# Retention's sample queries: weighted states summed by a matrix of ones, in place of a product with the query

## The chip, the cores and the metric

One Trainium2 chip, one of its cores. The time is the device time of one execution of the whole program in microseconds (us); several executions are timed, and their median is given. A core has TensorE (PE; its weight loads are listed as PEld), VectorE (DVE), ScalarE (ACT), GpSimd (POOL) and SyncE (SP), each with an instruction queue of its own that it works through in order. Engines wait for one another by semaphores. SP issues nearly all DMAs here.

## The reference

One step of a decoder layer for a prompt (16 meta tokens and 256 prompt tokens) and for 8 samples that each add one token to a state of their own. The layer is a half feed-forward block, a mixer of two parallel branches (retention with 8 heads, HGRN2 with 16) and a second half feed-forward block. What the change touches is retention of the 8 samples, for which a chunk has one token:

```python
q_dec = q * jnp.exp(lg[:, None] * (idx + 1.0))[:, :, None]
o = jnp.einsum('bhij,bhjv->bhiv', inner, v) + jnp.einsum('bhid,bhdv->bhiv', q_dec, S)
S_new = jnp.exp(lg * C)[:, None, None] * S + jnp.einsum('bhjd,bhjv->bhdv', k_dec, v)
```

With one token both terms of `o` together are the query times the new state: o[v] = sum over d of q[d] * S_new[d, v], with d = 256 features and v = 256 values, for each of 8 heads and 8 samples.

## The kernel before

All matrices are float32. A weight block of 128x128 is split into a high part `whi` (ScalarE's cast, L188) and a low part `wlo` (VectorE's difference, L189), and each product is three matmuls (`xh*whi`, `xl*whi`, `xh*wlo`, L218). Weights come in units of 8 blocks, 512 KB, through three buffers each of `raw`, `whi` and `wlo`: the load of a unit waits for the wlo of the unit three before, and its cast for TensorE's last use of the unit three before.

The mixer's projections run over the heads u = 0 to 7: six groups f, q_h, i_h, q_r, k_r, v_r (names of the parts of `w_in`) of head u, then four gate groups of head u - 1 (`g_r` with `a_r`, `g_h` with `a_h`, for each of two columns of 128). A group is two outputs, 16 k-steps of six matmuls each, four units of weights. When a group's matmuls are issued, `evacuate` takes its result out of PSUM: for a gate group ScalarE makes the sigmoid of `g`, later the sigmoid of `a`, both into tiles named `gs`, and VectorE multiplies them (`gt`, `y`).

Between the k-steps run the two branches as Python generators, `mix_hg(u)` and `mix_ret(u)`. Each `yield n` means: go on n k-steps later (`pump`). TensorE's order is just the order in which the program issues its matmuls; the order of the other engines is set by a scheduler with priorities, in which the weights' casts and differences come first.

`mix_ret(u)` holds the samples' states of a head in four tiles `sms` (tag `smr`), for samples 0 to 3 and 4 to 7 (e) and for both halves of the features (c), each 128 partitions x 4 samples x 256 values. ScalarE scales them by the decay (L1192), VectorE adds key times value (`smr<-vbr,k_r,smr`, L1198), and SP writes them out (`out_srs`). Then, 19 k-steps later for u of 1 and more, TensorE multiplies the states by the queries: `qdr` is a tile of zeros with one query column per sample, 32 columns wide, so that a matmul writes 32 rows of which one is the answer; four samples go side by side into four groups of 32 rows (`tile_position`), into the PSUM tile `pqr`. VectorE's `alone` places the queries in `qdr`. In `mix_hg` the corresponding product `pq` (L1039) is placed by `yield (8, 11, 45)[min(u, 2)]` so that from u = 2 on it comes right before `pqr`. After `pqr` come its centring, and 7 k-steps on the outputs `por` and the normalisation. The first use of the normalised result is in the gate groups of the same head, one round of projections later.

The heads u = 2 to 7 are alike; their `pqr` stands in the third gate group (of head u - 1), after k-step 11. In u = 0 it stands in the group q_r, in u = 1 at the end of the gate groups.

Of the kernel before, what the change touches and what calls it, by code (L numbers as in the profile page):

```python
# [13 lines left out]
AF = mybir.ActivationFunctionType  # L14
ALU = mybir.AluOpType
# [3 lines left out]
P = 128  # L19
# [4 lines left out]
NMETA, SEQ, NS = 16, 256, 8  # L24
# [27 lines left out]
ALONE = 4 * 32 + 1  # L52
# [76 lines left out]
def trunk(ctx: ExitStack, tc: tile.TileContext, A, O):  # L129
    nc = tc.nc  # L130
# [108 lines left out]
    def mul(out, a, b):  # L239
        nc.vector.tensor_tensor(out=out, in0=a, in1=b, op=ALU.mult)  # L240
# [306 lines left out]
    with tc.tile_pool(name="yp", bufs=1) as yp:  # L547
# [7 lines left out]
        with tc.tile_pool(name="mp", bufs=1) as mp:  # L555
# [7 lines left out]
            def tmp(name, shape=(P, T), bufs=1, dt=F32, tag=None):  # L563
                if name in rows:
                    rows[name] = rows[name][1:] + rows[name][:1]
                    return rp.tile(list(shape), dt, tag=rows[name][-1], name=name)
                return mp.tile(list(shape), dt, tag=tag or name, name=name, bufs=bufs)
# [16 lines left out]
            st = {}  # L584
# [5 lines left out]
            qdr = tmp("qdr", (P, 4, ALONE))  # L590
            nc.gpsimd.memset(qdh, 0.0)
            nc.gpsimd.memset(qdr, 0.0)
            qdh_at = [qdh.rearrange("p a c -> p (a c)")[:, 256 * h :] for h in range(2)]
            qdr_at = [qdr.rearrange("p a c -> p (a c)")[:, 2 * ALONE * c :] for c in range(2)]
# [53 lines left out]
            def evacuate(n, c0, c1, o0, o1, b0, b1):  # L648
                if n == "f":
# [6 lines left out]
                    st["f"], st["k"] = f, k  # L656
                elif n == "q_h":
# [4 lines left out]
                    st["q"] = q  # L662
                elif n == "i_h":
# [23 lines left out]
                elif n in ("g_r", "g_h"):  # L687
# [5 lines left out]
                    nc.scalar.activation(sa, o1, AF.Sigmoid)  # L693
                    mul(t, t, sa)
# [38 lines left out]
            def alone(qd, q):  # L733
                nc.vector.tensor_copy(
                    qd[:, :, : 128 : 32].rearrange("p (c e) j -> p c e j", e=2),
                    q[:, :, SEQ:].rearrange("p c (e j) -> p c e j", e=2))
# [9 lines left out]
            def mix_hg(u, f, k, q, v):  # L746

                calm = 2
# [285 lines left out]
                yield (8, 11, 45)[min(u, 2)]  # L1034
# [50 lines left out]
            def mix_ret(u, q, k, v):  # L1085
# [47 lines left out]
                alone(qdr, q)  # L1133
# [70 lines left out]
                yield (11 if u == 0 else 15) + 2 * calm  # L1204
                pq = mx_bank("pqr")
                scores(pq[:, 256:], 2)
                for e in range(2):
                    for c in range(2):
                        for j in range(4):
                            b = 4 * e + j  # L1210
                            nc.tensor.matmul(  # L1211
                                pq[32 * j : 32 * j + 32, :256], qdr_at[c][:, 32 * b : 32 * b + 32],
                                sms[2 * e + c][:, j, :], start=e + c == 0, stop=e + c == 2, tile_position=(0, 32 * j))
# [163 lines left out]
```

## Time and profile before

| | us |
|---|---|
| median of 3 timed runs | 2566.84 (2566.56 to 2567.51) |
| profiled execution, span from first to last instruction | 2563.9 |
| TensorE busy in the span | 2553.4 |
| VectorE busy | 1702.8 |
| ScalarE busy | 1392.2 |
| GpSimd busy | 57.0 |
| mixer, 746 to 1703: VectorE busy of 957 | 776.4 |

The profiled execution has no other time beside its span; the span is 2.9 shorter than the median of the timed runs. In the lines of the profile a row names line, engine, operation, and "written <- read" tiles with shapes (partitions x elements); what stands in brackets at the end of a timeline row is how long the engine had been idle and what released it. TensorE's granted clock is full (1.000) throughout.

### The profile page before, as it was taken

The numbers are of one execution on the slowest core, as the hardware profiler recorded it, in microseconds if no ns is written. First come the engines' busy times: TensorE is split into PE (matmuls) and PEld (weight loads), VectorE is DVE, ScalarE is ACT, GpSimd is POOL, SyncE is SP. The second block draws the span as 40 slices with busy tenths as digits, with TensorE's granted clock in tenths as the row PEclk, the third lists the DMA queues.
The fourth block names the chain that finished last, engine by engine and source line by source line (L and its number), as shares of the span: only waits on it lengthen the run. The fifth ranks groups of instructions, "written<-read, shape, count | busy, mean of one in ns | idle before, by whom it ended". The sixth has DMA issues, their size and how long they took to land.

```text
span 2563.9 us, 56275 instructions
## 1 busy us (share of the span) xinstructions
PE 2553.4 (100%) x23424; PEld 2534.4 (99%) x23424; DVE 1702.8 (66%) x2827; ACT 1392.2 (54%) x2186; POOL 57.0 (2%) x152
## 2 busy tenths in 40 slices
PE   9999999999999999999999999999999999999999
PEld 9999999999999999999999999999999999999998
DVE  6444544475569878777777777777885555556555
ACT  5444444444456767767676666675564444444443
POOL 0000000000000000000000000000000000000000
PEclk9999999999999999999999999999999999999999
DMA  7555555555555876767676767675556565565554
GB/s 244 183 187 183 187 182 184 186 182 186 184 201 180 287 265 232 264 214 260 212 264 215 259 223 255 224 239 188 196 190 197 194 197 195 194 196 195 195 195 149
DMA packets 156897, 536.26 MB, mean 209 GB/s; under 512 B 17952, under 2 KB 25952, under 8 KB 156640
## 3 DMA queue, kind: packets, MB, share of 16 engines
q1 hardware_dynamic: 156352, 532.37, 62.0%
q8 instruction: 183, 3.00, 0.5%
q14 instruction: 74, 0.61, 0.1%
q10 hardware_dynamic: 288, 0.29, 0.0%
HBM read 501.99 MB, written 30.61 MB: 208 GB/s over the span
## 4 chain that ended last, share of the span: by engine, by line
PE 96%; DVE 2%; ACT 0%; issue 0%; DMA 0%; SPq 0%; ACTq 0%; DVEq 0%
PE up L218 36%; PE dn L218 19%; PE pj_i_h L218 3%; PE pj_g_r L218 3%; PE pj_q_h L218 3%; PE pj_g_h L218 3%; PE pj_a_r L218 3%; PE pj_a_h L218 3%; PE pj_f L218 3%; PE pj_q_r L218 3%; PE pj_k_r L218 3%; PE wo L218 3%; PE pj_v_r L218 3%; DVE wlo L189 1%; PE pqr L1211 1%; PE psr L1168 0%
## 5 line engine op out<-in xcount | busy, mean ns | idle before, releaser
L189 DVE TENSOR_TENSOR wlo<-raw,whi 128x1024 fp32r<-128x1024 f32 (+1 forms) x869 | 1062.2, 1223 | 740.7 <-ACT whi L188 737.3
L188 ACT CAST whi<-raw 128x1024 fp32r<-128x1024 f32 (+1 forms) x870 | 905.7, 1042 | 909.2 <-PE up L218 411.0
L218 PE MATMUL up<-xh,whi 128*128 128x280 f32 (+1 forms) x2624 | 725.6, 280 | 0.6 <-ACT whi L188 0.6
L218 PE MATMUL up<-xh,wlo 128*128 128x280 f32 (+1 forms) x2624 | 725.8, 280 | 0.4 <-DVE wlo L189 0.3
L218 PE MATMUL up<-xl,whi 128*128 128x280 f32 (+1 forms) x2624 | 725.4, 279 | 0.0
L218 PEld LDWEIGHTS up<-xh,wlo 128*128 128x128 f32 x2624 | 492.6, 189 | 1.0 <-DVE wlo L189 1.0
L218 PEld LDWEIGHTS up<-xh,whi 128*128 128x128 f32 x2624 | 492.6, 189 | 0.8 <-ACT whi L188 0.8
L218 PEld LDWEIGHTS up<-xl,whi 128*128 128x128 f32 x2624 | 492.6, 189 | 0.0
L218 PE MATMUL dn<-hh,whi 128*128 128x280 f32 (+1 forms) x1376 | 384.7, 280 | 0.0
L218 PE MATMUL dn<-hh,wlo 128*128 128x280 f32 (+1 forms) x1376 | 384.3, 279 | 0.0
L218 PE MATMUL dn<-hl,whi 128*128 128x280 f32 (+1 forms) x1376 | 384.3, 279 | 0.0
L218 PEld LDWEIGHTS dn<-hh,whi 128*128 128x128 f32 x1376 | 260.1, 189 | 0.1
L218 PEld LDWEIGHTS dn<-hl,whi 128*128 128x128 f32 x1376 | 260.1, 189 | 0.1
L218 PEld LDWEIGHTS dn<-hh,wlo 128*128 128x128 f32 x1376 | 260.1, 189 | 0.0
L218 PE MATMUL pj_k_r<-xh,whi 128*128 128x280 f32 x256 | 74.2, 290 | 0.0
L218 PE MATMUL pj_g_r<-xh,whi 128*128 128x264 f32 x256 | 74.0, 289 | 0.0
L218 PE MATMUL pj_v_r<-xh,whi 128*128 128x280 f32 x256 | 73.8, 288 | 0.0
L218 PE MATMUL pj_v_r<-xh,wlo 128*128 128x280 f32 x256 | 72.4, 283 | 0.3 <-DVE wlo L189 0.3
L218 PE MATMUL pj_g_h<-xh,whi 128*128 128x264 f32 x256 | 72.7, 284 | 0.0
L218 PE MATMUL pj_k_r<-xh,wlo 128*128 128x280 f32 x256 | 72.4, 283 | 0.0
L218 PE MATMUL pj_v_r<-xl,whi 128*128 128x280 f32 x256 | 72.3, 283 | 0.0
L218 PE MATMUL pj_k_r<-xl,whi 128*128 128x280 f32 x256 | 72.3, 283 | 0.0
(421 smaller groups left out, 5263.4 us busy)
## 6 DMA issues: line engine op xcount, KB each, us to landing
raw<-in_w_up SPq DMA_DIRECT2D x343, 512.0 KB, 4.1
raw<-in_w_in SPq DMA_DIRECT2D x320, 512.0 KB, 4.3
raw<-in_w_dn SPq DMA_DIRECT2D x172, 512.0 KB, 3.5
smr<-in_sr SPq DMA_DIRECT2D x32, 512.0 KB, 5.0
out_srs<-smr SPq DMA_DIRECT2D x32, 512.0 KB, 6.7
raw<-in_w_out SPq DMA_DIRECT2D x32, 512.0 KB, 3.9
vbr<-vrd SPq DMA_DIRECT2D x32, 256.0 KB, 4.1
smh<-in_sg SPq DMA_DIRECT2D x16, 512.0 KB, 5.2
```

The costliest lines, as they stand in the source:

```text
L188: nc.scalar.copy(hi[:, j:jn, :], raw[:, j:jn, :])
L189: nc.vector.tensor_tensor(out=lo[:, j0:j1, :], in0=raw[:, j0:j1, :], in1=hi[:, j0:j1, :].bitcast(F32), op=ALU.subtract)
L218: nc.tensor.matmul(o, w, t, start=start, stop=stop)
L1211: nc.tensor.matmul(pq[32 * j : 32 * j + 32, :256], qdr_at[c][:, 32 * b : 32 * b + 32], sms[2 * e + c][:, j, :], start=e + c == 0, stop=e + ...
```

## The change

In `mix_ret` the product with the queries is taken apart. The state's rows are weighted by the query before TensorE sees them: for samples 0 to 3 GpSimd multiplies half c = 0 by the query of its feature (a scalar per partition), for samples 4 to 7 ScalarE does; VectorE then multiplies half c = 1 by its query and adds. Both work in place, in the tiles that have been written out. What is left is a sum over 128 partitions, for which TensorE multiplies by a column of ones (`one`, again 32 columns wide): 8 matmuls of the same shape per head in place of 16.

GpSimd first copies one element of the tile `seen` (the output of the evacuation that came last, in the gate groups the sigmoid of `a`) into `lq`, then the queries over it: so the weighting can't begin before that evacuation. The weighting is issued 25 k-steps after the states' writing out, the product 8 k-steps later, 33 in all where there were 19 (15 for u = 0). In `mix_hg`, `pq` moves by the same 14 steps (45 to 59).

```diff
--- before.py
+++ after.py
@@ -587,11 +587,12 @@
 
 
             qdh = tmp("qdh", (P, 4, ALONE))
-            qdr = tmp("qdr", (P, 4, ALONE))
+            one = tmp("one", (P, 2, 32))
             nc.gpsimd.memset(qdh, 0.0)
-            nc.gpsimd.memset(qdr, 0.0)
+            nc.gpsimd.memset(one, 0.0)
+            for e in range(2):
+                nc.gpsimd.memset(one[:, e, e : e + 1], 1.0)
             qdh_at = [qdh.rearrange("p a c -> p (a c)")[:, 256 * h :] for h in range(2)]
-            qdr_at = [qdr.rearrange("p a c -> p (a c)")[:, 2 * ALONE * c :] for c in range(2)]
             vsm = tmp("vsm", (P, P))
             vt2 = tmp("vt2", (P, 2, P))
             scr2 = tmp("scr2", (P, NMETA))
@@ -654,12 +655,14 @@
                         nc.scalar.activation(f[:, j, :], f[:, j, :], AF.Identity, scale=olb[:, c : c + 1], bias=lb[:, c : c + 1])
                     nc.scalar.activation(k, f, AF.Identity, scale=-1.0, bias=1.0)
                     st["f"], st["k"] = f, k
+                    st["seen"] = f[:, 0, :]
                 elif n == "q_h":
                     q = tmp("q", (P, 2, TL))
                     for j, (o, b) in enumerate(((o0, b0), (o1, b1))):
                         nc.scalar.activation(q[:, j, :], o, AF.Sigmoid, **bias(b))
                         mul_biased(q[:, j, :], o, b, q[:, j, :])
                     st["q"] = q
+                    st["seen"] = q[:, 0, :]
                 elif n == "i_h":
                     v = st.pop("i_h", None)
                     if v is None:
@@ -691,6 +694,7 @@
                     mul(t, sg, o0)
                     sa = tmp("gs", (P, TL), bufs=2)
                     nc.scalar.activation(sa, o1, AF.Sigmoid)
+                    st["seen"] = sa
                     mul(t, t, sa)
                     u, e = divmod(c0, 2)
                     while u not in (done_r if n == "g_r" else done_h):
@@ -1031,7 +1035,7 @@
                 if u == 1:
                     yield 2
                     samples(1)
-                yield (8, 11, 45)[min(u, 2)]
+                yield (8, 11, 59)[min(u, 2)]
                 pq = mx_bank("pq")
                 for h in range(2):
                     for b in range(NS):
@@ -1130,7 +1134,6 @@
                         nc.vector.scalar_tensor_tensor(
                             out=lo, in0=x, scalar=g, in1=his[i].bitcast(F32), op0=ALU.mult, op1=ALU.subtract)
                     yield 2
-                alone(qdr, q)
                 vts = [vt[:, 0], vt[:, 1], vs2]
                 vrow = rows_out(vt2.rearrange("p c f -> p (c f)")[16:24, :], 256, "vr")
 
@@ -1201,16 +1204,28 @@
                     for c in range(2):
                         nc.sync.dma_start(O["srs"][u, c, :, 4 * e : 4 * e + 4, :], ss[c])
                     yield 1 if e else 10 if u == 0 else 6
-                yield (11 if u == 0 else 15) + 2 * calm
+                yield 25
+                late_q = tmp("lq", (P, 2, NS))
+                nc.gpsimd.tensor_copy(late_q[:, 0, :1], st["seen"][:, :1])
+                nc.gpsimd.tensor_copy(late_q, q[:, :, SEQ:])
+                for e in range(2):
+                    s0, s1 = sms[2 * e : 2 * e + 2]
+                    for b in range(4):
+                        g = [late_q[:, c, 4 * e + b : 4 * e + b + 1] for c in range(2)]
+                        if e:
+                            nc.scalar.activation(s0[:, b, :], s0[:, b, :], AF.Copy, scale=g[0])
+                        else:
+                            nc.gpsimd.tensor_scalar(out=s0[:, b, :], in0=s0[:, b, :], scalar1=g[0], scalar2=None, op0=ALU.mult)
+                        nc.vector.scalar_tensor_tensor(
+                            out=s0[:, b, :], in0=s1[:, b, :], scalar=g[1], in1=s0[:, b, :], op0=ALU.mult, op1=ALU.add)
+                yield 8
                 pq = mx_bank("pqr")
                 scores(pq[:, 256:], 2)
                 for e in range(2):
-                    for c in range(2):
-                        for j in range(4):
-                            b = 4 * e + j
-                            nc.tensor.matmul(
-                                pq[32 * j : 32 * j + 32, :256], qdr_at[c][:, 32 * b : 32 * b + 32],
-                                sms[2 * e + c][:, j, :], start=e + c == 0, stop=e + c == 2, tile_position=(0, 32 * j))
+                    for j in range(4):
+                        nc.tensor.matmul(
+                            pq[32 * j : 32 * j + 32, :256], one[:, e, :], sms[2 * e][:, j, :],
+                            start=e == 0, stop=e == 1, tile_position=(0, 32 * j))
                 mul(scr2[:NB2], pq[:NB2, 256 : 256 + NMETA], dt[:NB2, c2:])
                 upper_upper_lower(sc2, scr2[:NB2])
                 os = tmp("osr", (P, 256))
```

ScalarE's queue at the end of the third gate group, u = 3 (`whi` with a number is a weight unit's cast, in brackets what the instruction waits for), before:

```order
L1217 COPY osr<-pqr 128x256 [waits PE_49]
L188 CAST whi_15464<-raw_15463 128x8x128 [waits DMAHW7_49,PE_49,Activation_49]
L690 ACTIVATE gs<-pj_g_r_15213 128x264 [waits PE_49]
L188 CAST whi_15494<-raw_15493 128x8x128 [waits DMAHW1_49,PE_49,Activation_49]
L693 ACTIVATE gs<-pj_a_r_15214 128x264 [waits PE_49]
L1055 ACTIVATE sqh<-po 128x256 [waits DVE_49]
```

and with the change:

```order
L188 CAST whi_15427<-raw_15426 128x8x128 [waits DMAHW7_49,DVE_49,PE_49]
L693 ACTIVATE gs<-pj_g_r_15244 128x264 [waits PE_49]
L188 CAST whi_15457<-raw_15456 128x8x128 [waits DMAHW1_49,DVE_49,PE_49]
L696 ACTIVATE gs<-pj_a_r_15245 128x264 [waits PE_49]
L1216 ACTIVATE smr<-smr,lq 128x256 [waits DMAHW0_49,Pool_49]
L1216 ACTIVATE smr<-smr,lq 128x256 x3
L188 CAST whi_15527<-raw_15526 128x8x128 [waits DMAHW3_49,DVE_49,PE_49]
```

The casts around both sigmoids stay where they were; the four products stand behind the second sigmoid and ahead of the next cast, and wait for GpSimd's `lq` and for a DMA that writes states out.

VectorE's queue at the same place, before:

```order
L189 TENSOR_TENSOR wlo_15465<-raw_15463,whi_15464 128x8x128 [waits DMAHW7_49,PE_49,Activation_49]
L240 TENSOR_TENSOR gt<-gs,pj_g_r_15213 128x264 [waits Activation_49]
L189 TENSOR_TENSOR wlo_15495<-raw_15493,whi_15494 128x8x128 [waits DMAHW1_49,PE_49,Activation_49]
L240 TENSOR_TENSOR gt<-gt,gs 128x264 [waits DVE_49,Activation_49]
L742 COPY on_h<-po 128x2x8 [waits PE_49]
L240 TENSOR_TENSOR y<-gt,on_r 128x264 [waits DVE_49]
```

and with the change:

```order
L189 TENSOR_TENSOR wlo_15458<-raw_15456,whi_15457 128x8x128 [waits DMAHW1_49,PE_49,Activation_49]
L240 TENSOR_TENSOR gt<-gt,gs 128x264 [waits DVE_49,Activation_49]
L1219 SCALAR_TENSOR_TENSOR smr<-smr,lq 128x256 [waits DMAHW3_49,Pool_49]
L240 TENSOR_TENSOR y<-gt,on_r 128x264 [waits DVE_49]
L1219 SCALAR_TENSOR_TENSOR smr<-smr,lq 128x256 [waits Pool_49] x3
L189 TENSOR_TENSOR wlo_15528<-raw_15526,whi_15527 128x8x128 [waits DMAHW3_49,PE_49,Activation_49]
L1219 SCALAR_TENSOR_TENSOR smr<-smr,lq 128x256 [waits DMAHW0_49]
L1219 SCALAR_TENSOR_TENSOR smr<-smr,lq 128x256 x3
L189 TENSOR_TENSOR wlo_15593<-raw_15591,whi_15592 128x8x128 [waits DMAHW4_49,PE_49,Activation_49]
```

The eight sums come behind gt, four ahead of a unit's wlo and four behind it; a sum of the first four waits for GpSimd's product.

TensorE's queue around the sample products of u = 3, before (third gate group, after k-step 11, `xh_10` being the eleventh chunk of x):

```order
L218 MATMUL pj_a_r_15214<-xh_10_9275,wlo_15277 128x264
L1039 MATMUL pq<-smh,qdh 32x128 [waits DMAHW5_49]
L1039 MATMUL pq<-smh,qdh 32x128 x7
L1039 MATMUL pq<-smh,qdh 32x128 [waits DMAHW1_49]
L1039 MATMUL pq<-smh,qdh 32x128 x7
L1141 MATMUL pqr<-q_r,k_r 16x16 x2
L1211 MATMUL pqr<-smr,qdr 32x256 x16
L218 MATMUL pj_g_r_15213<-xh_11_9279,whi_15276 128x264
```

and with the change (fourth gate group, after k-step 9, one k-step into the unit whose cast stood between the two sigmoids):

```order
L218 MATMUL pj_a_h_15376<-xh_8_9269,wlo_15458 128x264
L1043 MATMUL pq<-smh,qdh 32x128 [waits DMAHW5_49]
L1043 MATMUL pq<-smh,qdh 32x128 x7
L1043 MATMUL pq<-smh,qdh 32x128 [waits DMAHW1_49]
L1043 MATMUL pq<-smh,qdh 32x128 x7
L1144 MATMUL pqr<-q_r,k_r 16x16 x2
L1226 MATMUL pqr<-smr,one 32x256 [waits DVE_49] x8
L218 MATMUL pj_g_h_15375<-xh_9_9273,whi_15457 128x264
```

Both products moved together by 14 k-steps, half of the retention matmuls are gone, and the others wait for VectorE.

## The prediction

> **What bounds the kernel now.** I read the page first: span, busy shares, chain.
>
> ```profile
> span 2563.9 us, 56275 instructions
> PE 2553.4 (100%) x23424; PEld 2534.4 (99%) x23424; DVE 1702.8 (66%) x2827; ACT 1392.2 (54%) x2186; POOL 57.0 (2%) x152
> PE 96%; DVE 2%; ACT 0%; issue 0%; DMA 0%; SPq 0%; ACTq 0%; DVEq 0%
> ```
>
> TensorE is the bound for nearly the whole span. The list of TensorE's own waits (total, times, longest) says how little the others have held it up so far: nine rows, 4.4 us together, of which these are the first two and the last.
>
> ```profile
> PE pw L515 <- DVE eps_h L163: 1.0, 1, 1.0
> PE pt L1116 <- POOL tails L1103: 0.9, 1, 0.9
> ...
> PE wo L218 <- DVE yl L226: 0.2, 1, 0.2
> ```
>
> So a microsecond of TensorE's work taken away is won, and a microsecond for which TensorE is made to wait is lost. The change does both, once a head. The profiled span of 2563.9 us is 2.9 (0.1%) below the median of 2566.84, and I add my sum to the median. Less than 0.2%, 5.1 us, can't be told from no change here.
>
> Next I took one head apart, the fourth (u = 3), in the timelines (start, duration, what). TensorE:
>
> ```profile
> 1190.44 0.28 PE L218 MATMUL pj_a_r<-xh,wlo 128*128 128x264 f32 x1
> 1190.65 1.08 PE L1039 MATMUL pq<-smh,qdh 128*32 128x128 f32 x32
> ...
> 1191.60 0.42 PE L1211 MATMUL pqr<-smr,qdr 128*32 128x256 f32 x3
> ...
> 1193.47 0.38 PE L218 MATMUL pj_g_r<-xh,whi 128*128 128x264 f32 x1
> ...
> 1196.28 0.28 PE L218 MATMUL pj_g_r<-xh,whi 128*128 128x264 f32 x1
> ...
> 1196.95 0.28 PE L218 MATMUL pj_g_h<-xh,whi 128*128 128x264 f32 x1
> ```
>
> The HGRN2 sample product (`pq`) and the retention one (`pqr`) stand side by side in the third of the four gate groups; one k-step of six matmuls lasts 0.67 (1196.28 to 1196.95); the fourth gate group begins at 1196.95. ScalarE and VectorE at the same place:
>
> ```profile
> 1191.48 1.05 ACT L188 CAST whi<-raw 128x1024 fp32r<-128x1024 f32 x1 [1.41 <-DMA raw<-in_w_in]
> ...
> 1194.94 1.05 ACT L188 CAST whi<-raw 128x1024 fp32r<-128x1024 f32 x1 [0.23 <-DMA raw<-in_w_in]
> 1196.81 0.39 ACT L690 ACTIVATE gs<-pj_g_r 128x264 f32<-128x264 f32 x1 [0.83 <-PE pj_g_r L218]
> 1197.39 1.04 ACT L188 CAST whi<-raw 128x1024 fp32r<-128x1024 f32 x1 [0.19 <-DMA raw<-in_w_in]
> 1198.35 0.38 ACT L693 ACTIVATE gs<-pj_a_r 128x264 f32<-128x264 f32 x1
> ```
>
> ```profile
> 1198.47 1.23 DVE L189 TENSOR_TENSOR wlo<-raw,whi 128x1024 fp32r<-128x1024 f32 x1 [0.81 <-ACT whi L188]
> 1199.61 0.43 DVE L240 TENSOR_TENSOR gt<-gt,gs 128x264 f32<-128x264 f32 x1
> ...
> 1200.08 0.43 DVE L240 TENSOR_TENSOR y<-gt,on_r 128x264 f32<-128x264 f32 x1
> 1200.43 0.16 DVE L240 TENSOR_TENSOR sqh<-on_h 128x8 f32<-128x8 f32 x1
> ```
>
> Three weight casts in a row were released by a DMA's landing and not by TensorE: the weight stream is late here. The table by stretch says why (its last cells are clock, share of the DMA engines' time, GB/s), and so do the issues with their median time to landing, first of 1178 to 1202 us, then of the whole run: the sample states come in and go out at this place, and a weight load takes 5.8 us against 4.3.
>
> ```profile
> 1190.00:1202.00 12.00, 12.00 (x147) 10.85 (x146) 8.23 (x18) 6.50 (x15) 0.00 (x0) 1.00 0.95 335
> ```
>
> ```profile
> raw<-in_w_in SPq DMA_DIRECT2D x8, 512.0 KB, 5.8
> ...
> raw<-in_w_in SPq DMA_DIRECT2D x320, 512.0 KB, 4.3
> ```
>
> **The matmuls removed.** Sixteen per head become eight of the same shape. Sixteen last from 1191.60 to 1193.47, 1.87 us; half is 0.93, and all of it is TensorE's path. Eight heads: **-7.4 us**.
>
> **When TensorE asks for the sums.** With `pq` and `pqr` gone from the third gate group (1190.55, where the step ended, to 1193.47: 2.92 us), TensorE begins the fourth group at 1196.95 - 2.92 = 1194.03. Nine steps follow (9 x 0.67 = 6.03), then `pq` and the scores as before (1190.55 to 1191.60: 1.05). It asks for the first four sums at 1201.1, and half of 0.93 later, at **1201.6**, for the last four.
>
> **When they are ready.** GpSimd's first new copy waits for the sigmoid of `pj_a_r` (the tile `seen`). In ScalarE's new order that sigmoid still stands behind the weight cast which the DMA released at 1197.39, and the DMA doesn't land sooner because TensorE is early: its issue hangs on earlier wlos, which hang on earlier landings. So the sigmoid ends at 1198.73 as now. That is 4.7 after the new start of the fourth group, when TensorE has done seven of the nine steps; 2.9 us are left to 1201.6. What must still pass, in VectorE's new order, is the rest of this wlo and gt (to 1200.04), one sum, y, three sums, the next unit's wlo, four sums. Sums of this shape exist, back to back:
>
> ```profile
> 1298.91 2.07 DVE L1198 SCALAR_TENSOR_TENSOR smr<-vbr,k_r,smr 128x256 f32<-128x256 f32 x5 [1.27 <-ACT smr L1192]
> ```
>
> Five in 2.07 is 0.40 from start to start. A wlo takes 1.14 to the next start (1198.47 to 1199.61), y 0.35 (1200.08 to 1200.43). Eight sums, y and wlo are 8 x 0.40 + 0.35 + 1.14 + 0.1 at the end = 4.8 us of VectorE alone, more than the 2.9 that are left. ScalarE's four products (as long as a sigmoid of 264 columns, 0.38) run beside the first sums, with the cast for that wlo behind them in its queue, and are no later than the wlo's turn.
>
> GpSimd's product of 128x256 is not in the trace. Its nearest rows, and one that tells more, with VectorE's row of the same moment:
>
> ```profile
> 745.21 0.53 POOL L591 MEMSET qdh<- 128x516 f32 x1 [743.95 <-PE dn L218]
> ...
> 832.22 0.28 POOL L1174 TENSOR_SCALAR gam<-sro 128x1 f32<-128x1 f32 x1
> ...
> 1296.51 1.18 POOL L1174 TENSOR_SCALAR gam<-sro 128x1 f32<-128x1 f32 x1 [9.91 <-ACT sro L1170]
> ```
>
> ```profile
> 1296.43 1.21 DVE L189 TENSOR_TENSOR wlo<-raw,whi 128x1024 fp32r<-128x1024 f32 x1
> ```
>
> A memset of twice the columns takes 0.53, so 256 columns are worth some 0.2, and with 0.28 for one column I take 0.45. But that same one-column instruction takes 1.18 when a wlo runs, and ends at 1297.69, just behind the wlo's 1297.64: GpSimd is held while VectorE reads.
>
> Three prices for this head follow.
> - Free: first product done at 1199.7, VectorE starts its sums right after gt, at 1200.04, and ends at 1204.9; TensorE waits 1204.9 + 0.1 - 1201.6 = 3.4.
> - Copies held: the copy that falls into wlo and gt ends with them, at 1200.1, the second at 1200.4, the first product at 1200.85; plus 4.8 is 1205.7: a wait of 4.2.
> - All held: products and sums also exclude each other, so 4 x 0.45 stands in one line with VectorE's first five: 1200.4 + 1.8 + 1.95, wlo 1.14, four sums 1.7: 1207.0, a wait of 5.5.
>
> I take the middle one: the row at 1296.51 shows a small instruction held, and no row shows a 128x256 one that holds or is held. For the other five late heads (u = 2 and 4 to 7), whose order is the same, this is how far the cast may come sooner; ScalarE's row and the issue of its load in u = 2:
>
> ```profile
> 1070.76 1.04 ACT L188 CAST whi<-raw 128x1024 fp32r<-128x1024 f32 x1
> ```
>
> ```profile
> 1064.37 0.33 SPq L185 DMA_DIRECT2D raw<-in_w_in  x1
> ```
>
> 1064.37 + 5.8 = 1070.2, so TensorE's lead would bring the cast forward by 0.6 at most. With half of that, six heads wait 3.9 each: **+23.4 us** (ends, from free less 0.7 to all held: +16 and +33).
>
> The Trainium skill goes further than the row at 1296.51. The page "SBUF — State Buffer", section "Who interferes with whom", says that a VectorE instruction with two SBUF inputs and a GpSimd instruction that reads SBUF contend for one port, and the later one is blocked in full. The trace agrees as far as it goes (1.18 against 0.28). By that rule every new product stands against every new sum: "all held", below.
>
> **The first two heads.** In the first (u = 0) `seen` is long done, but ScalarE's products wait until the states of samples 4 to 7 are written out, and a weight cast waits behind them:
>
> ```profile
> 854.47 0.80 SPq L1202 DMA_DIRECT2D out_srs<-smr  x1
> ...
> out_srs<-smr SPq DMA_DIRECT2D x32, 512.0 KB, 6.7
> ```
>
> ```profile
> 859.89 1.05 ACT L188 CAST whi<-raw 128x1024 fp32r<-128x1024 f32 x1 [0.83 <-DMA raw<-in_w_in]
> ```
>
> 854.47 + 6.7 = 861.2; four products, two copies, cast from some 863.3 instead of 859.89. TensorE has about two units of weights (2.7 us each) ahead of it there, which covers part: +1.5 (ends 0 and 2.5). In the second head (u = 1) fourteen steps lie between the last gate group and the sums instead of nine, 3.4 us more: 0.
>
> **Smaller edits.** VectorE loses eight small copies (`alone`) and gains 64 x 0.40 = 26 us; outside these places its 66% leave gaps. GpSimd's memsets come before the projections. `pq` and both normalisations move by 14 steps; the gates that use them come 80 steps or more after the sums, in the last head 4 to 12 after the norms. On SP's queue the next head's two state loads now wait for the last sums; behind them are weight loads that are needed three units later, which covers 1.6 us.
>
> **The sum.** 2566.84 - 7.4 + 23.4 + 1.5 = 2584.3.
>
> **Rivals.** Hidden (the other side): the sums are done when TensorE comes, 2566.84 - 7.4 = 2559.4. It needs the sigmoid about 4 us sooner, so weights that land as if no states moved beside them; it decides at a wait of 0.93 a head. For it: eight sums are only 3.2 us, and 2 or 3 units are buffered. Against: three casts in a row released by DMAs that were issued long before. Even: weights land up to 2 us sooner and no copy is held, waits of 0.5 to 2 in six heads and none in the first: 2562 to 2572. All held: 2566.84 - 7.4 + 33 + 2.5 = 2595; for it speaks 1.18 against 0.28. Each product behind a whole wlo, as at 1296.51: beyond 2600; against it, only one wlo stands among them. That the eight matmuls save nothing is not likely: nothing else fills TensorE between 1191.60 and 1193.47.
>
> **How the numbers follow.** Forecast (2572 to 2590) 0.56; all held 0.17; beyond 2600 0.04; even 0.12; hidden 0.11. Slower by over 0.2% is the first three, 0.77; within 0.2% is even, 0.12; faster is hidden, 0.11. The range 2567 to 2600 leaves out hidden, the lower part of even and the last: under 0.2.
>
> **What would show it.** A new row among TensorE's waits, `pqr` L1226 on VectorE `smr`, six times or more at about 4 us; `pqr` itself 0.9 a head; GpSimd's copy of `seen` drawn out over the wlo; the cast ahead of the sigmoid still released by a DMA. If these casts follow TensorE at once, "when they are ready" is wrong and 2560 to 2572 comes out; if GpSimd's products take 1 us and more, "all held" or worse.

## The result, and the profile after

The changed kernel takes 2610.07 us (median of 4, 2609.76 to 2613.35), the kernel before 2566.70 beside it: a ratio of 1.0172, 95% interval 1.0157 to 1.0186. It is slower, as forecast, but by 43 us and not by 17.5. The profiled execution's span is 2608.5, 44.6 more than before. The page of the changed kernel: span, busy shares, chain.

```profile
span 2608.5 us, 56165 instructions
PE 2574.9 (99%) x23296; PEld 2539.2 (97%) x23296; DVE 1733.4 (66%) x2883; ACT 1402.3 (54%) x2216; POOL 100.3 (4%) x202
PE 85%; DVE 6%; DMA 4%; ACT 2%; POOL 1%; issue 1%; SPq 0%; ACTq 0%; DVEq 0%; POOLq 0%
```

VectorE, DMA, ScalarE and GpSimd now hold 13% of the chain, where they had 2%. TensorE is listed as busier although it has less to do; that is told below (the clock). Its own waits and, in the second fence, those of its weight loads (total, times, longest):

```profile
PE pqr L1226 <- DVE smr L1219: 9.1, 18, 0.9
PE pj_q_r L218 <- ACT whi L188: 4.8, 1, 4.8
PE pst L1026 <- DVE km L255: 2.3, 1, 2.3
PE pj_f L218 <- DVE wlo L189: 2.0, 2, 1.4
```

```profile
PEld pqr L1226 <- DVE smr L1219: 26.0, 44, 1.4
```

The forecast row is there, and most of it stands with the weight loads: the `one` columns for each matmul are loaded only when the sum is ready. (The two rows overlap in time and must not be added.) The next rows were not forecast; they are single waits in the first two heads, of which only 0.7 of the last row was there before.

Some names in these and later rows: `osr` is the copy of the result `pqr` that VectorE centres, and `por` turns it; `pst` is a product of the HGRN2 branch that reads `km`, which VectorE makes; `pt` turns small tiles, among them `ends`, which GpSimd copies.

To divide the 44.6 us I take the start of the same matmul in both traces, the first of the third gate group ahead of the sums, or of the very last group. Before:

```profile
924.63 0.28 PE L218 MATMUL pj_g_r<-xh,whi 128*128 128x264 f32 x1
...
1056.79 0.28 PE L218 MATMUL pj_g_r<-xh,whi 128*128 128x264 f32 x1
...
1749.85 0.28 PE L218 MATMUL pj_g_h<-xh,whi 128*128 128x264 f32 x1
```

and with the change:

```profile
933.80 0.28 PE L218 MATMUL pj_g_r<-xh,whi 128*128 128x264 f32 x1
...
1072.18 0.28 PE L218 MATMUL pj_g_r<-xh,whi 128*128 128x264 f32 x1
...
1794.42 0.28 PE L218 MATMUL pj_g_h<-xh,whi 128*128 128x264 f32 x1
```

The lag is 9.2 us after head 0, 15.4 after head 1 and 44.6 at the end: **15.4 us in the first two heads, 29.2 in the six late ones.** The same two lags of every experiment stand in the table of the next section.

**A late head** (u = 3), in the timelines of GpSimd, ScalarE, VectorE and TensorE:

```profile
1218.24 0.95 POOL L1209 COPY lq<-gs 128x1 f32<-128x1 f32 x1 [25.50 <-ACT gs L696]
...
1219.64 3.69 POOL L1218 TENSOR_SCALAR smr<-smr,lq 128x256 f32<-128x256 f32 x4
...
1216.84 1.05 ACT L188 CAST whi<-raw 128x1024 fp32r<-128x1024 f32 x1 [1.17 <-DMA raw<-in_w_in]
1217.79 0.38 ACT L696 ACTIVATE gs<-pj_a_r 128x264 f32<-128x264 f32 x1
...
1217.92 1.23 DVE L189 TENSOR_TENSOR wlo<-raw,whi 128x1024 fp32r<-128x1024 f32 x1 [0.94 <-ACT whi L188]
...
1220.60 0.69 DVE L1219 SCALAR_TENSOR_TENSOR smr<-smr,lq 128x256 f32<-128x256 f32 x1 [1.11 <-POOL smr L1218]
...
1223.36 0.48 DVE L1219 SCALAR_TENSOR_TENSOR smr<-smr,lq 128x256 f32<-128x256 f32 x1 [0.21 <-POOL smr L1218]
1223.77 1.22 DVE L189 TENSOR_TENSOR wlo<-raw,whi 128x1024 fp32r<-128x1024 f32 x1
1224.90 1.67 DVE L1219 SCALAR_TENSOR_TENSOR smr<-smr,lq 128x256 f32<-128x256 f32 x4
...
1221.39 0.60 PE L1226 MATMUL pqr<-smr,one 128*32 128x256 f32 x2
...
1225.43 1.81 PE L1226 MATMUL pqr<-smr,one 128*32 128x256 f32 x8 [0.91 <-DVE smr L1219]
1227.17 0.38 PE L218 MATMUL pj_g_h<-xh,whi 128*128 128x264 f32 x1
```

The sigmoid (`gs`) ends at 1218.17; only then can GpSimd's copy of it begin, and behind it the products. The four products take 0.92 from start to start (3.69 for four), each of the first four sums waits for its product, the wlo follows, then the last four sums, which end at 1226.57. TensorE is ready at 1221.39. Without a wait the projection would have gone on 0.93 later, at 1222.3; it went on at 1227.17: 4.9 us lost.

**Head 0**, GpSimd, SP, ScalarE and TensorE:

```profile
851.74 5.32 POOL L1218 TENSOR_SCALAR smr<-smr,lq 128x256 f32<-128x256 f32 x4 [1.22 <-DMA out_srs<-smr]
857.01 1.11 POOL L773 COPY smh<-acch 128x1 f32<-128x1 f32 x1
...
858.15 0.33 SPq L774 DMA_DIRECT2D smh<-in_sg  x1
858.59 0.37 SPq L185 DMA_DIRECT2D raw<-in_w_in  x1
859.00 0.43 SPq L1205 DMA_DIRECT2D out_srs<-smr  x1
...
865.36 1.71 ACT L1216 ACTIVATE smr<-smr,lq 128x256 f32<-128x256 f32 x4 [5.49 <-DMA out_srs<-smr]
...
867.77 1.05 ACT L188 CAST whi<-raw 128x1024 fp32r<-128x1024 f32 x1
...
868.88 0.59 PE L218 MATMUL pj_q_r<-xh,whi 128*128 128x264 f32 x1 [4.83 <-ACT whi L188]
```

and the same copy of one column before, then SP's wait for it in the changed kernel:

```profile
851.89 0.30 POOL L769 COPY smh<-acch 128x1 f32<-128x1 f32 x1 [18.11 <-DVE acch L836]
```

```profile
SPq L774 <- POOL smh L773: 7.1, 1, 7.1
```

Five links: GpSimd's products hold back a one-column copy; SP's load of an HGRN2 state waits for that copy; behind it on SP stand a weight load and the writing out of the states; ScalarE's products wait for the writing out; the weight cast stands behind them.

**The clock.** The table by stretch, 1 us each (TensorE busy first; after the engines the granted clock):

```profile
867.00:868.00 1.00, 0.00 (x0) 0.00 (x0) 0.68 (x3) 1.00 (x4) 0.25 (x1) 0.75 1.00 360
868.00:869.00 1.00, 0.12 (x1) 0.13 (x1) 0.94 (x3) 1.00 (x2) 0.00 (x0) 0.50 1.05 430
...
873.00:874.00 1.00, 1.00 (x6) 1.00 (x6) 0.97 (x4) 0.95 (x5) 0.00 (x0) 0.50 0.86 119
874.00:875.00 1.00, 1.00 (x10) 1.00 (x9) 0.94 (x4) 0.39 (x2) 0.00 (x0) 0.84 0.76 287
...
974.00:975.00 1.00, 1.00 (x6) 0.85 (x5) 0.80 (x3) 0.98 (x2) 0.00 (x0) 0.50 0.46 123
```

The granted clock falls to 0.50 at 867.5, still in the stall, and stays there until 874.3: 6 matmuls start in a us instead of 10 to 12. That is why TensorE "gains" busy time. Some 5 us of these were work at half clock, so 2.5 us are lost. In head 1 the idle time is 1.4 (wlo) and 2.3 (`pst`, whose km stands on VectorE behind five sums, 970.10 to 972.16, and a wlo); the clock is at half from 973.3 to 980.1, about 3.2 lost.

### The profile page after: what moved, and what is told of

The parts are those of the page before. It is cut to its first block, busy times and chain, and to the rows that moved or that the text cites. A ratio compares the mean times of both kernels' runs of the same rounds, so it can differ in the third digit from the quotient of the medians.

```text
span 2608.5 us, 56165 instructions
## 1 busy us (share of the span) xinstructions
PE 2574.9 (99%) x23296; PEld 2539.2 (97%) x23296; DVE 1733.4 (66%) x2883; ACT 1402.3 (54%) x2216; POOL 100.3 (4%) x202
## 4 chain that ended last, share of the span: by engine, by line
PE 85%; DVE 6%; DMA 4%; ACT 2%; POOL 1%; issue 1%; SPq 0%; ACTq 0%; DVEq 0%; POOLq 0%
PE up L218 36%; PE dn L218 18%; PE pj_v_r L218 3%; PE wo L218 3%; PE pj_q_h L218 3%; PE pj_f L218 3%; PE pj_q_r L218 3%; PE pj_i_h L218 3%; PE pj_k_r L218 3%; DMA raw<-in_w_in 3%; DVE wlo L189 3%; PE pj_g_r L218 2%; PE pj_a_r L218 2%; PE pj_g_h L218 1%; PE pj_a_h L218 1%
## 5 line engine op out<-in xcount | busy, mean ns | idle before, releaser
L218 PE MATMUL pj_g_h<-xh,wlo 128*128 128x264 f32 x256 | 71.2, 278 | 1.9 <-DVE wlo L189 1.9
```

The source lines that it names most:

```text
L218: nc.tensor.matmul(o, w, t, start=start, stop=stop)
```

## The experiments

Lags as above, from the profiled executions; medians and ratios from the timed runs. A profiled execution of a kernel with long waits can lie some us from its median (f4: span 2599.9, runs 2601.68 to 2608.21), and a lag of one profile is no better than some 3 us: f1, f4, h3 and h5 leave the late heads as in the changed kernel and show 25.9 to 27.0 where that shows 29.2. In f1, h2 and h5 1.3 to 1.6 us of the lag given for heads 0 and 1 are there at 745 us already, ahead of the mixer's first matmul.

| kernel | median us | ratio, 95% interval | heads 0, 1 | heads 2 to 7 |
|---|---|---|---|---|
| changed | 2610.1 | 1.0157 to 1.0186 | 15.4 | 29.2 |
| e1 ones alone | 2562.3 | 0.9972 to 0.9991 | -0.4 | -2.6 |
| e2 move alone | 2573.7 | 1.0016 to 1.0035 | 4.8 | 2.9 |
| h4 ones, moved | 2572.1 | 1.0009 to 1.0028 | 5.4 | -1.5 |
| f1 late heads only | 2594.3 | 1.0089 to 1.0119 | 1.9 | 27.0 |
| f2 first heads only | 2581.4 | 1.0037 to 1.0071 | 16.6 | 0.2 |
| e3 products on VectorE | 2618.2 | 1.0186 to 1.0217 | 13.6 | 39.7 |
| e4 no copy of seen | 2589.2 | 1.0074 to 1.0104 | 11.9 | 10.3 |
| g1 short products | 2596.7 | 1.0098 to 1.0128 | 11.4 | 19.6 |
| h2 no copy, short | 2584.4 | 1.0048 to 1.0082 | 11.3 | 8.4 |
| h1 no sums | 2597.3 | 1.0105 to 1.0135 | 10.3 | 19.8 |
| f3 late ask | 2602.1 | 1.0125 to 1.0155 | 13.6 | 21.8 |
| g5 late ask, short | 2592.8 | 1.0084 to 1.0115 | 9.9 | 13.4 |
| g4 three together | 2595.2 | 1.0092 to 1.0125 | 8.6 | 21.9 |
| g3 next gate, heads 2 to 6 | 2574.9 | 1.0021 to 1.0043 | 0.7 | 7.0 |
| f4 first heads later | 2607.5 | 1.0137 to 1.0168 | 9.2 | 26.8 |
| h3 head 0 without ScalarE | 2607.8 | 1.0144 to 1.0174 | 15.3 | 25.9 |
| h5 head 0, copies moved | 2605.5 | 1.0133 to 1.0167 | 14.1 | 26.5 |

**What the parts make without the weighting.** e1: no weighting, old places.

```diff
-                yield (8, 11, 59)[min(u, 2)]
+                yield (8, 11, 45)[min(u, 2)]
...
-                yield 25
-                late_q = tmp("lq", (P, 2, NS))
...
-                yield 8
+                yield (11 if u == 0 else 15) + 2 * calm
```

> The weighting is left out: the 8 matmuls by ones sum the states as they are, at the place of before (so the sample outputs lack the query). Only the matmuls removed and the eight small copies of alone are left of the change. Late sums (my theory: the loss is all waiting for the weighting, the matmuls themselves save 0.93 a head): 2566.8 - 7.4 = 2559.4, 2557.5 to 2561. Rival, the saved matmuls are worth nothing because the weight stream limits TensorE at that place: 2566 to 2568.

It is faster by 4.8 us (0.9981): each head gains 0.87, and some is given back, since TensorE then meets weights that are late (two waits of the gate groups for wlo, 1.2 us in all). e2: only the places, in the kernel before.

```diff
-                yield (8, 11, 45)[min(u, 2)]
+                yield (8, 11, 59)[min(u, 2)]
...
-                yield (11 if u == 0 else 15) + 2 * calm
+                yield 33
```

> The kernel before with nothing but the two places moved: pqr 33 steps after the states' writing out, pq by yield 59; 16 matmuls with the queries as before. Late sums: the move alone costs nothing, 2566.8, 2565 to 2570. Rival, the place: pq and pqr no longer give the weight loads 2.9 us in the third gate group, TensorE runs into the weights there, and most of the 43 us would be there without the weighting: 2585 or more. Between: 1.7 and 1.2 us that the third group of two heads lost in the changed kernel, 2570 to 2573.

It is 6.6 us slower: neither nothing nor most of the 43, and just above the case between. The first two heads carry 4.8 of 7.7. (The 1.7 and 1.2 us of the changed kernel that are named above stand in the second gate group of two heads, not in the third.) h4 has both parts.

```diff
-                yield 25
-                late_q = tmp("lq", (P, 2, NS))
...
-                yield 8
+                yield 33
```

> Eight matmuls by ones and both places moved as in the changed kernel, no weighting (the query is left out). Both parts add up: 2567.1 - 4.9 (matmuls alone) + 6.6 (move alone) = 2568.8, 2566 to 2572. Rival (the move's cost came from 16 matmuls at the new place, and eight fit): 2562 to 2565.

The result is 2572.1, 4.7 above before and at the upper end of the range: the parts add up within 3 us, and the eight matmuls don't pay for the move. In head 0 `por` waits 3.1 us for `osr`, and the clock is at half for 3.4 us from the end of that wait. The weighting itself thus costs 2610.1 - 2572.1 = 38 us.

**Which heads.** Weighting for some heads, the others with queries and old places (f1 as shown, f2 with `u < 2`).

```diff
+                weigh = u >= 2
...
-                yield 25
+                yield 25 if weigh else (11 if u == 0 else 15) + 2 * calm
```

> The change for the heads 2 to 7 only; heads 0 and 1 keep the 16 matmuls with the queries at their old places. By the starts of the groups in the changed kernel's trace the heads 2 to 7 make 29.2 of its 44.6 us: 2566.8 + 29.2 = 2596, 2590 to 2600. Rival (my prediction's share: the first two heads cost 1.5 less 1.9, everything lies in the late heads): 2608 or more.

> The change for the heads 0 and 1 only; heads 2 to 7 as before. By the changed kernel's trace these two make 15.4 us, of which some 9.3 are TensorE idle (weights behind ScalarE's products in head 0, km behind VectorE's sums in head 1) and some 6.7 half clock after it, less 1.9 for the matmuls: 2566.8 + 15.4 = 2582, 2577 to 2586. Rival (my prediction's share): 2566 to 2569.

They lose 27.2 and 14.3 us: 41.5 of 43.4, so the two shares add up within 2 us, and the first two heads are a third of the loss. The rival, my prediction's share, falls.

**Who paces a late head.** e3: GpSimd's products to VectorE.

```diff
-                            nc.gpsimd.tensor_scalar(out=s0[:, b, :], in0=s0[:, b, :], scalar1=g[0], scalar2=None, op0=ALU.mult)
+                            nc.vector.tensor_scalar(out=s0[:, b, :], in0=s0[:, b, :], scalar1=g[0], scalar2=None, op0=ALU.mult)
```

> GpSimd's four products a head go to VectorE, all else as in the changed kernel. Late sums: a product of 128x256 with one input takes VectorE 0.3 to 0.4 (between its copy of 16 columns, 0.17, and its two-input 0.40 to 0.48) in place of 0.92 on GpSimd, the four products no longer set the pace of the first four sums, and in a late head the last sum ends about 1 us sooner: -6; in the second head GpSimd's copy for km is no longer behind the products: -2 to -6 with the half clock behind it. 2596 to 2603. Rival (the pace is not GpSimd's, only the place or the late sigmoid counts): 2608 to 2613, slower if anything since VectorE does more.

The expectation was wrong: it is 8 us slower than the changed kernel, though a product takes 0.35. The group of the products, and VectorE's timeline of u = 3:

```profile
L1218 DVE TENSOR_SCALAR smr<-smr,lq x32: 344/349/356, 853.4 to 1756.2; 128x256 f32<-128x256 f32 x32
```

```profile
1221.38 1.22 DVE L189 TENSOR_TENSOR wlo<-raw,whi 128x1024 fp32r<-128x1024 f32 x1 [0.66 <-ACT whi L188]
1222.53 0.48 DVE L1219 SCALAR_TENSOR_TENSOR smr<-smr,lq 128x256 f32<-128x256 f32 x1
...
1223.98 1.22 DVE L189 TENSOR_TENSOR wlo<-raw,whi 128x1024 fp32r<-128x1024 f32 x1
1225.11 1.27 DVE L1219 SCALAR_TENSOR_TENSOR smr<-smr,lq 128x256 f32<-128x256 f32 x3
```

Two sums stand ahead of this; the scheduler put one wlo ahead of the third sum and a second among the others; with a wait of 0.66 for a cast the last sum ends at 1226.38, hardly sooner. In u = 2 and from u = 4 on the waits are longer (up to 1.7 in one piece, against 0.9), and the clock falls there: five stretches at 0.50, 23.9 us in all (from 1356.6 to 1363.4, for instance), in which TensorE worked for some 22 us and so lost 11. That is as much as the 10.5 by which the late heads are slower than in the changed kernel. So e3 doesn't tell what GpSimd's pace costs: its products add to VectorE's work, and the clock covers the rest. e4: without the copy of `seen`, the gate that holds the weighting until the sigmoid.

```diff
-                nc.gpsimd.tensor_copy(late_q[:, 0, :1], st["seen"][:, :1])
```

> GpSimd's copy of the tile seen is left out, so the weighting of samples 0 to 3 may begin when their states are written out (landed at 1210.2 in the fourth head, where the sigmoid ended at 1218.2), the other four when theirs are (1218.0). Late sums: the first four are done before TensorE comes, the last four end near 1221 instead of 1226.6; five of the late heads' 5 us go, the first two heads stay: 2610 - 24 to 30, 2580 to 2586. Rival, a new block: ScalarE's products wait for the DMA of the written states with a weight cast behind them, as in the first head, and TensorE waits for weights instead: 2600 or more.

The time falls by 20.8 us, that of the late heads from 29.2 to 10.3: the result lies between the two ranges, nearer the first, and of all single edits this one brings most. In head 1, too, `pst` now waits 0.5 at most instead of 2.3, and the half clock there is gone. What is left is a new wait, as the rival had it but in size far smaller:

```profile
PE pj_g_r L218 <- DVE wlo L189: 7.7, 6, 2.7
```

g1: the products shortened, nothing else.

```diff
-                            nc.gpsimd.tensor_scalar(out=s0[:, b, :], in0=s0[:, b, :], scalar1=g[0], scalar2=None, op0=ALU.mult)
+                            nc.gpsimd.tensor_scalar(out=s0[:, b, :32], in0=s0[:, b, :32], scalar1=g[0], scalar2=None, op0=ALU.mult)
```

> The changed kernel with GpSimd's products on 32 of the 256 columns (the weighting of the other 224 is left out for samples 0 to 3, half c = 0); every other instruction stays. GpSimd's pace: the products take about 0.3 in place of 0.92, the first four sums follow at 0.40 instead of 0.92, the wlo behind them and the last four sums come 1.5 to 2 us sooner in each of six late heads: 2610 - 9 to 12, 2598 to 2601. Rival (VectorE's own queue and the casts are the limit, as the products on VectorE at 0.35 brought nothing): 2607 to 2611.

The time falls by 13.4 us, 9.6 of it in the late heads: GpSimd's pace costs 1.6 a head (1.0 if the changed kernel's late heads are put at 25.9, as in h3). This is the first theory, with a result a little below its range. h2 has both edits.

> The copy of seen left out and GpSimd's products on 32 of 256 columns. Without the copy TensorE waited 7.7 us for wlo in the third group of the six late heads. GpSimd's pace (that wlo stands behind sums that wait for products of 0.92): most of that goes, 2589 - 5 to 8, 2581 to 2584. Rival (that wlo waits for a cast behind ScalarE's products, which wait for the written states' DMA): 2587 to 2590.

The result is 2584.4, 4.8 below e4 and just above the first theory's range. The wait for wlo in the third group falls from 7.7 to 3.3, but that in the fourth group rises from 1.3 to 3.8; the late heads gain only 1.9, which is within the scatter of one profile. So what the pace costs with the gate gone is not settled. h1: no sums on VectorE.

```diff
-                        nc.vector.scalar_tensor_tensor(
-                            out=s0[:, b, :], in0=s1[:, b, :], scalar=g[1], in1=s0[:, b, :], op0=ALU.mult, op1=ALU.add)
```

> The changed kernel without VectorE's 64 sums (half c = 1 is left out of the sample outputs); TensorE waits for the products alone. Sums on VectorE: in a late head the last product ends at 1223.3 where the last sum ended at 1226.6, 3.1 less for six heads, and no wlo stands behind sums; in head 1 km no longer stands behind five sums, another 4 to 7: 2610 - 19 - 4 to 7 = 2584 to 2588. Rival (GpSimd and its gate alone): 2600 or more.

The result is 2597.3, between the theories and nearer the rival. Even with no sum to make, gate and GpSimd alone keep 19.8 of the 29.2.

**A later place.** f3: the matmuls 12 steps later.

```diff
-                yield 8
+                yield 20 if 2 <= u < HR - 1 else 8
```

> The changed kernel with the eight matmuls 12 k-steps (8 us) later in the heads 2 to 6; the weighting itself stays where it is. Late sums (TensorE waits only because it asks 5 us before VectorE has the last sum): five heads lose their wait, 2610 - 25 = 2585, 2582 to 2592. Rival (the engines' queues are what is short, so that TensorE waits for wlo or the casts instead, wherever pqr stands): 2600 or more.

It gains only 8.0, and the rival is right in kind. TensorE's wait for the sums is left in head 7 alone (1.5), but two other rows have come; the timelines of u = 3 show the first (ScalarE's casts, then VectorE):

```profile
PE pj_g_h L218 <- DVE wlo L189: 8.0, 7, 1.7
PE pt L882 <- POOL ends L755: 4.7, 5, 0.9
```

```profile
1218.40 1.98 ACT L188 CAST whi<-raw 128x1024 fp32r<-128x1024 f32 x2
...
1220.57 0.48 DVE L1219 SCALAR_TENSOR_TENSOR smr<-smr,lq 128x256 f32<-128x256 f32 x1 [0.21 <-POOL smr L1218]
1220.97 1.22 DVE L189 TENSOR_TENSOR wlo<-raw,whi 128x1024 fp32r<-128x1024 f32 x1
```

The first cast was done at 1219.43; its wlo starts at 1220.97, since it stands behind four sums that GpSimd paces. Most of the loss only changed its place. g5 is f3 with short products:

> GpSimd's products on 32 of 256 columns and the matmuls 12 k-steps later in the heads 2 to 6. GpSimd's pace: in the late-ask kernel TensorE waited for a wlo that stood behind the four paced sums (cast done 1219.43, wlo 1220.97 in the fourth head); with short products that wlo comes at once, and five heads lose most of what they still wait: 2602 - 8 to 15, 2587 to 2594. Rival (the late ask left what VectorE's and the DMA's load cost there): 2600 to 2603.

It is 9.3 below f3, the late heads fall from 21.8 to 13.4, and the wait of `pj_g_h` for wlo from 8.0 to 1.3: that reading holds. g4 is e4, f4 (below) and f3 together:

> Three of the edits together: no copy of seen, the first two heads later (10 and 6 steps), the matmuls 12 steps later in heads 2 to 6. If each works on its own wait: 2610 - 21 (seen) - 3 to 9 (first heads) = 2580 to 2586, the late ask adding 0 to 5 more, since without the copy TensorE waits for wlo in the third group and not for the sums: 2576 to 2586. Rival (the gains add up, 21 + 3 + 8): 2573 to 2578, still slower than before.

The expectation was wrong: it is 6 us slower than e4 alone. The edits don't add; with the matmuls later, the late heads lose 21.9 instead of 10.3. Its rows for wlo in the third group (8.1 us), for `pt` (4.7) and for head 0's cast (5.0) stand side by side; why head 0's stall and a half clock in head 2 came with them stays open. g3: heads 2 to 6 only, weighted behind the last sigmoid of the round, summed in the next (the edit is shown against the changed kernel).

```diff
+                weigh = 2 <= u < HR - 1
...
-                yield 25
+                yield 41 if weigh else (11 if u == 0 else 15) + 2 * calm
...
-                yield 8
+                if weigh:
+                    yield 20
```

> The change for the heads 2 to 6 only, weighted one evacuation later (behind the last sigmoid of the round, where the states have long landed) and summed by TensorE in the next round; heads 0, 1 and 7 as before, pq as before. If all is a matter of the place, where states and weights share the DMA and VectorE's wlo is what TensorE waits for: 2567 - 5 x 0.87 = 2562.7, 2560 to 2566. Rival (GpSimd's pace ahead of wlo costs wherever it stands, 1.5 a head): 2568 to 2574.

```profile
PE pj_q_h L218 <- DVE wlo L189: 4.3, 5, 0.9
```

It is 7.8 us slower than before: the rival, a little beyond its range. The written states have long landed here, though SP issues the next head's two state loads in the midst of it (1220.5 in u = 3), and TensorE still waits for a wlo in each of the five heads. At none of the three places (third group, fourth, next round) does the weighting pass unseen, and no version that computes all of it beats the kernel before.

**Head 0's chain.** f4: weighting and matmuls later in heads 0 and 1.

```diff
-                yield 25
+                yield 35 if u == 0 else 31 if u == 1 else 25
```

> The changed kernel with weighting and matmuls 10 k-steps later in head 0 and 6 later in head 1. Blocked queue (in head 0 ScalarE's products wait for the DMA of the written states and the weight cast waits behind them; in head 1 the sums stand ahead of km on VectorE): by then the states are out and km is done, the idle 9.3 and the half clock behind it go, what the move itself costs stays: 2596 to 2601. Rival (the first two heads are short of engines, not badly ordered; the block comes at another cast): 2605 to 2612.

In the profiled execution the first two heads lose 9.2 instead of 15.4, with head 0's stall down from 4.8 to 1.8 and no half clock behind it; the median of the runs fell by 2.6 only. So the first theory holds in kind for head 0, and its size is not decided. For head 1 it fails: the products still follow the sigmoid, `pst` waits 2.3 as before, and the half clock stays (966.8 to 973.6). h3: head 0 without ScalarE's products.

```diff
-                        if e:
+                        if e and u:
                             nc.scalar.activation(s0[:, b, :], s0[:, b, :], AF.Copy, scale=g[0])
```

> In head 0 alone GpSimd does all eight products and ScalarE none; the rest as changed. Blocked queue (ScalarE's first product waits for the DMA of the written states, 865.3, with a weight cast behind it): TensorE's 4.8 us and the 3.3 of half clock go, 2610 - 8 = 2602, 2598 to 2606. Rival (the wait passes on: GpSimd's copies for the states of HGRN2 now stand behind its products): 2607 to 2612.

The result is 2607.8, the rival in kind: the wait passed on to VectorE's wlo, behind sums that now wait for GpSimd:

```profile
PE pj_q_r L218 <- DVE wlo L189: 5.8, 1, 5.8
```

So ScalarE's place is a link and not the first. h5: in head 0 the one-column copies leave GpSimd's queue.

```diff
-                    nc.gpsimd.tensor_copy(sms[h][:, 0, :1], kts[0][:, 0, :1] if h else acc[:, 15:16])
+                    (nc.gpsimd if u else nc.vector).tensor_copy(sms[h][:, 0, :1], kts[0][:, 0, :1] if h else acc[:, 15:16])
...
-                    nc.gpsimd.tensor_copy(vbs[h][:, 0, :1], kts[1][:, 0, :1] if h else acc[:, 2 * P + 15 : 2 * P + 16])
+                    (nc.gpsimd if u else nc.vector).tensor_copy(vbs[h][:, 0, :1], kts[1][:, 0, :1] if h else acc[:, 2 * P + 15 : 2 * P + 16])
```

> In head 0 alone the four one-column copies (L773, L777) for which SP's loads of the HGRN2 states wait go from GpSimd to VectorE; the rest as changed. GpSimd's queue as the head of the chain (products 851.74 to 857.06, the copy behind them, SP's load waiting for it 7.1 us, behind that on SP a weight load and the writing out, for which ScalarE's products wait, with a weight cast behind them): SP is 4 to 5 us sooner, TensorE's 4.8 and the 3.3 of half clock behind it go, 2610 - 8 = 2602, 2599 to 2605. Rival (SP's queue is not the head; the states' writing out is late for VectorE's sake): 2608 to 2612.

SP's wait and TensorE's, in the first heads:

```profile
SPq L774 <- DVE smh L773: 2.1, 1, 2.1
```

```profile
PE pj_q_r L218 <- ACT whi L188: 2.0, 1, 2.0
```

7.1 became 2.1 and 4.8 became 2.0: the copy behind GpSimd's products is the first link. The median fell by 4.6, about half of what was expected, and not all of that is this edit's: the first two heads lose 12.5 without the 1.6 that stand there ahead of the mixer, 2.9 less than in the changed kernel. The rest of the stall and half clocks of 3.4 us in both heads remain, and `por` now waits 2.1 for `osr` where it waited 1.0.

## Why the prediction was right or wrong

**Right in kind.** The sum named the late heads' wait for VectorE's sums, and it is there; the sigmoid stands behind a cast that a DMA released (1216.84, idle 1.17), and GpSimd's copy of `seen` is drawn out over the wlo (0.95).

**The matmuls removed** were put at -7.4. Alone they gave -4.8: the size on TensorE is right (0.87 a head), the weights took some of it back.

**When TensorE asks** was right: 1221.39 in the trace is 7.16 behind the group's start (1214.23), forecast 7.1.

**When they are ready** is the first step that was mis-sized. A GpSimd product was put at 0.45, from a memset and a one-column instruction; it takes 0.92. Sums beside products take 0.69 instead of 0.48. So the four sums and y take 3.25 (1220.60 to 1223.85) where 1.95 was worked out; the sigmoid came 0.8 sooner than forecast, and the wait is 4.9 where the price taken said 4.2 and the mean over the heads 3.9. Over six heads the lag of 29.2, with 6 x 0.93 saved, is 34.8 of waiting against 23.4 forecast, beyond "all held". I had written that 1 us and more a product would mean that; at 0.92 it did. About 31 of it is in the fourth group. The third group loses nothing: in each head it is 2.9 to 3.1 shorter, as forecast. The rest is single waits for late weights in other groups, the two longest (1.7 and 1.2) in second gate groups.

**The first two heads** is the step that failed: +1.5 and 0 forecast, 15.4 + 2 x 0.93 = 17.3 measured, over half of the miss. I had the row of the writing out (6.7) and ScalarE's place, but counted from 854.47, where SP issued the writing out before; in the changed kernel it was issued at 859.00, so ScalarE's products began at 865.36 instead of 861.2. I looked at GpSimd's queue only for the late heads, and did not ask what stands behind its products in head 0: the one-column copy for which SP waits (h5). In head 1 I counted steps, 14 instead of 9, and not what stands on VectorE behind the sums (km), once the gate has made them late (e4). And I had no term for the clock: 2.5 and 3.2 us are lost at half clock.

**Smaller edits.** The move, costed at nothing, costs 4.7 net of the matmuls saved (h4), and there all of it lies in the first two heads (5.4), where `por` waits for `osr`. So part of their 17.3 is the move's; how much is not shown, since in the changed kernel that wait is 1.0 and not 3.1.

**The rivals.** "All held" was right in its time for the late heads (33) and wrong in its mechanism, so that its time was luck: products and sums run beside each other. The Trainium skill, page "SBUF — State Buffer", section "Who interferes with whom", calls the shared port an exclusive lock, so that the later of two such instructions is blocked in full. The trace agrees one way only. GpSimd's instruction is held beside a wlo, and even where it came first: a product that began at 853.79, 0.16 before the wlo, took 2.08 (0.92 alone). But a sum that starts 0.06 behind a product ends 0.18 before it (1220.60 + 0.69, against 1220.54 + 0.93), held by 0.2 and not by 0.9.

## What to carry to other kernels

An instruction added to an idle engine is paid by whatever stands behind it in that engine's queue: follow each such instruction, down to one-column copies and the DMA queue that waits for them. That GpSimd was busy for 2% of the span said nothing about this; ask in each head, the first ones too, what comes next on that engine. And where TensorE is the bound, taking 0.9 us of its work a head away was no gain here, because the same VectorE makes the weights for it: time spent ahead of a wlo that TensorE needs soon came back as TensorE's wait (f3, g3).

## What the runs showed of the hardware

The same product of 128x256 float32 by a scalar per partition takes 0.92 on GpSimd, 0.49 on ScalarE and 0.35 on VectorE (e3). The groups of the changed kernel (minimum, median, maximum in ns), and of g1 with 32 columns:

```profile
L1218 POOL TENSOR_SCALAR smr<-smr,lq x32: 918/926/2085, 851.7 to 1748.1; 128x256 f32<-128x256 f32 x32
L1216 ACT ACTIVATE smr<-smr,lq x32: 492/495/510, 865.4 to 1746.5; 128x256 f32<-128x256 f32 x32
L1219 DVE SCALAR_TENSOR_TENSOR smr<-smr,lq x64: 470/481/696, 855.3 to 1751.8; 128x256 f32<-128x256 f32 x64
```

```profile
L1218 POOL TENSOR_SCALAR smr<-smr,lq x32: 362/640/1635, 850.1 to 1734.7; 128x32 f32<-128x32 f32 x32
```

By the shortest of each, from 0.362 for 32 columns to 0.918 for 256, a product costs 2.5 ns a column on top of some 0.28 (one column took that before). A memset's row (0.53 for 516 columns, 1 ns a column) was no measure for this instruction, which also reads.

TensorE's granted clock fell to 0.50 in a stall of 4.8 us, 3.4 us after its start, and also in the second of two stalls of 1.4 and 2.3 us within some 5 us; in the late heads of the changed kernel, with idle stretches of 0.3 to 0.9 among the matmuls, it stayed at 1.00. In all runs each stretch at half clock in the mixer lasted 3.4 or 6.8 us. The Trainium skill, page "TensorE: Matmul & The Clock Gate", section "Part 1: The HAM clock gate (the "warmup" mystery)", says that the clock goes to half after an idle window of about 3.4 us and comes back after as long a busy one, and that the windows run freely. The two values and the lengths agree with these rows. But no idle stretch of that length was needed: 3.7 us in two pieces were enough in head 1, and 1.7 and 0.8 us, one right after the other, in head 0 of g1, while 1.8 and 0.8 us in head 0 of f4 were not, which would fit windows that run freely.
